# Down projection with the activations stationary, the weights moving by 512 columns, and the sample's tokens apart in plain float32

## Chip, cores and metric

The kernel runs on one core of one Trainium2 chip. The metric is device time in microseconds of that core; two runs of the kernel before gave 1352.66 and 1353.6 us, median 1353.13.

## What is computed

One layer of a streaming encoder, one step for two requests: a prompt of 256 tokens and a sample of 32 tokens, width 2048. Both go through the same weights, all float32. The mixer (gated linear attention and forgetting attention) comes first and is untouched by the change; then comes the MLP with a hidden width of 8192:

```
h = RMSNorm_pre(x);  z = h @ w_in;  ... two groups of heads ...
x = x + RMSNorm_post(concat(gla_out, fox_out) @ w_out)
x = x + RMSNorm_post2(relu(RMSNorm_pre2(x) @ w_up)^2 @ w_down)
```

`w_up` is 2048 x 8192, `w_down` 8192 x 2048. RMSNorm divides each token by the root of its mean square over the 2048 channels and multiplies by a gain per channel. The attention's keys, values, gates and states are also outputs; the change doesn't touch them.

## The kernel before

All big products have one form, `gemm` (L182). The weights come in chunks of 512 columns by 2048 rows, each in eight pieces of 256 rows (two tiles of 128 rows, `KP` = 2), through a ring of four staging tiles (`wst`, L57) that SyncE's queue fills (L141). ScalarE rounds a piece to `whi` (float32r, L160) and VectorE subtracts to get the rest, `wlo` (L161): the weights' exact value in two parts of twelve bits. The activations are split the same way. For each of four output tiles and each tile of 128 rows, TensorE runs three products out of four (L198 hi x hi, L199 hi x lo, L200 lo x hi). **The weights are the stationary operand** (128 x 128, loaded anew for every product), and the activations of all 288 tokens, prompt and sample together, are the moving one. So a chunk is 8 x 4 x 2 x 3 = 192 products of 288 columns, and the result has channels on the partitions, tokens along the row. The four accumulators are four PSUM banks (`acc`); four more banks (`aux`) serve everything else.

The MLP (L923 on) goes through the hidden width in four blocks `b`: four chunks of `w_up` (L927), whose results are squared and split to `u_hi`, `u_lo` (L940 to L943), then four chunks of `w_down` (L953), whose results VectorE adds to `dT` (L960), sixteen tiles [128 channels, 288 tokens]. With the last block, each chunk's `dT` tiles are squared and summed for the norm (L786, L791, L970, `token_sums` L230), multiplied by the gain (L981) and turned to tokens on the partitions: TensorE transposes the prompt's two tiles (L985) and multiplies the sample's 32 columns by the identity into a quarter of the partitions of `psm` (L986, one of the four column groups of the array per chunk). `finish` (L992) scales by the token's factor `rt3` and adds the residual `yN`; `store` sends the rows out.

A tile scheduler sets the order of instructions on each engine from the program text, priorities (`soon`) and its own timing; staging and splitting run two to three pieces ahead of their use.

Of the kernel before, what the change touches and what calls it, by code (L numbers as in the profile page):

```python
# [15 lines left out]
P = 128  # L16
# [26 lines left out]
def hymba_step(  # L43
# [31 lines left out]
    # ------------------------------------------------------------- constants  # L75
# [29 lines left out]
    # ---------------------------------------------------- the weights' stream  # L105
    # chunks of CW columns, in pieces of KP rows of tiles; each piece is split exactly
    # into two parts of twelve bits, and three of the four products are taken
# [21 lines left out]
    staged, sent, ready, held = {}, {}, {}, {}  # held: what a piece's split stays behind  # L129

    def stage(i):
        """The weights' piece number i on its way from DRAM."""
        if i >= NP * len(chunks) or i in staged:
            return
        src, order = chunks[i // NP]
        k0 = order[i % NP] * KP
        st = wst.tile([P, KP, CW], F32, name="wstage", tag="wstage")
        n = 1 if i == 0 else KP
        with soon() if i >= NP else nullcontext():
            for a in range(0, KP, n):  # L140
                sent[i] = nc.sync.dma_start(out=st[:, a:a + n, :], in_=src[(k0 + a) * P:(k0 + a + n) * P, :]  # L141
                                            .rearrange("(k p) c -> p k c", p=P))
        staged[i] = st
# [38 lines left out]
    def gemm(ci, a_hi, a_lo, steps=1, ahead=2):  # L182
        """NO tiles of [128 columns of the weights, T]."""
# [20 lines left out]

    def act_tiles():
        hi = [actp.tile([P, T], F32R, name=f"ah{k}", tag=f"ah{k}") for k in range(KT)]
        lo = [actp.tile([P, T], F32R, name=f"al{k}", tag=f"al{k}") for k in range(KT)]
        return hi, lo

    def rstd(tile_, ms, n, out):  # L210
        """1/sqrt(ms/n + eps) from a sum of squares: exp(-ln/2) and a Newton step."""
        v, r, t = tile_(), tile_(), tile_()
        S.activation(out=r, in_=ms, func=AF.Ln, scale=1.0 / n, bias=eps_t)
        V.tensor_scalar(out=v, in0=ms, scalar1=1.0 / n, scalar2=EPS, op0=ALU.mult, op1=ALU.add)
        S.activation(out=r, in_=r, func=AF.Exp, scale=-0.5)
        V.scalar_tensor_tensor(out=t, in0=r, scalar=-0.5, in1=v, op0=ALU.mult, op1=ALU.mult)
        V.tensor_tensor(out=t, in0=t, in1=r, op=ALU.mult)
        V.scalar_tensor_tensor(out=out, in0=t, scalar=1.5, in1=r, op0=ALU.add, op1=ALU.mult)
# [4 lines left out]
    def broadcast_tokens(r, out):  # L223
        """A number per token, [128, 3] with tokens on the partitions, to every row of a [128, T] tile."""
# [5 lines left out]
    def token_sums(pn, parts):  # L230
        """Sums over the channels of [128, T] tiles, tokens on the partitions; the sample's tokens four times."""
# [16 lines left out]
    # ------------------------------------------------------------ token mixing  # L248
    with ExitStack() as zc:
# [8 lines left out]
        # ---- the input: transposed, times its gain  # L258
# [26 lines left out]
        def add_input(q):  # L285
            """Sums of squares of 512 of the input's channels."""
# [7 lines left out]
        def warm_up(n):  # L294
            """Keeps the tensor engine's clock up while the first loads are on their way."""
# [63 lines left out]
        # the narrow columns of w_in: gate rank and forget logits  # L359
# [9 lines left out]
        # sums the four groups of partitions that the narrow columns' products go to, and puts  # L369
        # the gate's rows in three places  # L370
# [6 lines left out]
        # the gate's second factor, split like the rest, its three products in one pass over the rows  # L377
# [9 lines left out]
        # masks  # L387
# [15 lines left out]
        # gate rank, forget gates and their running sums  # L403
# [3 lines left out]
        def log_sigmoid(out, in_, bias, n0, n1, w, pool_t):  # L407
            """min(x, 0) - log1p(exp(-|x|)) of x = in_ + bias, log1p with its rounding put right."""
# [18 lines left out]
        def small_tile():  # L427
# [18 lines left out]
            # logf of the new rows, tokens on the partitions  # L446
# [11 lines left out]
            # running sums: the prompt's, and the cache's with the new rows behind  # L458
# [30 lines left out]
        def to_tokens(src, dst):  # L489
            """A [128, T] tile's transpose to a [128, 3, 128] slice, tokens on the partitions."""  # L490
# [7 lines left out]
        # ---- gated linear attention, one head  # L498
        def gla_head(h):
# [23 lines left out]
            # the first chunk's keys decayed past the second, the last chunk's queries past the  # L523
            # third, and all keys decayed to the prompt's end
# [11 lines left out]
            # att^T: keys on the partitions  # L536
# [9 lines left out]
            # queries and the keys of earlier chunks  # L546
# [21 lines left out]
            # the final states  # L568
# [10 lines left out]
            # outputs, value channels on the partitions  # L579
# [87 lines left out]
        def fox_sample(g):  # L667
            """The new rows of four heads, one head to a quadrant of partitions."""
# [56 lines left out]
        def out_gate(k, acc):  # L725
            """The normed heads times silu(r)."""
# [47 lines left out]
    # ------------------------------------------------- output projection and MLP  # L774
# [5 lines left out]
    def add_square(total, src, first):  # L780
        """total += src^2, or total = src^2."""
# [12 lines left out]
    # x and y with tokens on the partitions: two tiles of the prompt, and the sample's  # L794
    # channels in four groups
# [7 lines left out]
    yT = [mp.tile([P, T], F32, name=f"yT{k}", tag=f"y{k}") for k in range(KT)]  # L803
# [95 lines left out]
    def residual():  # L899
        """The mixer's output, brought to tokens on the partitions, plus x."""  # L900
# [21 lines left out]
    dN = None  # L922
    for b in range(NB):  # L923
        u_hi = [mp.tile([P, T], F32R, name=f"uh{k}", tag=f"uh{k}") for k in range(KT)]
        u_lo = [resp.tile([P, T], F32R, name=f"ul{k}", tag=f"r{k}") for k in range(KT)]
        for j in range(NC):
# [5 lines left out]
            for o in range(NO):  # L932
# [9 lines left out]
                S.copy(out=u_hi[k], in_=u)  # L942
                V.tensor_tensor(out=u_lo[k], in0=u, in1=u_hi[k].bitcast(F32), op=ALU.subtract)  # L943
        drain()
        if b == 0:
            dT = [mp.tile([P, T], F32, name=f"dT{k}", tag=f"y{k}") for k in range(KT)]
        if b == NB - 1:
            sac3 = mp.tile([P, T], F32, name="sac3", tag="sac", bufs=2)
            dN = [mp.tile([P, D], F32, name=f"dN{t}", tag=f"n{t}") for t in range(2)]
            psm = aux()  # L950
            last = []
        for j in range(NC):
            accs = gemm(ci, u_hi, u_lo)  # L953
            ci += 1
            for o in range(NO):
                k = NO * j + o
                if b == 0:
                    V.tensor_copy(out=dT[k], in_=accs[o][:, 0:T])
                else:
                    V.tensor_tensor(out=dT[k], in0=accs[o][:, 0:T], in1=dT[k], op=ALU.add)  # L960
            if b < NB - 1:
                continue
            for o in range(NO):
                k = NO * j + o
                if j < NC - 1:
                    add_square(sac3, dT[k], k == 0)
                else:
                    q = square(dT[k])
                    if o < NO - 2:
                        V.tensor_tensor(out=sac3, in0=sac3, in1=q, op=ALU.add)  # L970
                    else:
                        last.append(q)
            if j == NC - 1:
                pn = aux()
                token_sums(pn, [sac3] + last)
                rt3 = tok_tile()
                rstd(tok_tile, pn[:, 0:3], D, rt3)
            for o in range(NO):
                k = NO * j + o
                dg = tmp()  # L980
                V.tensor_scalar_mul(out=dg, in0=dT[k], scalar1=vcol("mpost", k))  # L981
                if o == 0:
                    pd = [aux(), aux()]
                for t in range(2):
                    PE.transpose(out=pd[t][:, o * P:(o + 1) * P], in_=dg[:, t * P:(t + 1) * P], identity=ident)  # L985
                PE.matmul(out=psm[32 * j:32 * j + DEC, o * P:(o + 1) * P], lhsT=dg[:, SEQ:T], rhs=ident,  # L986
                          start=True, stop=True)
            if j < NC - 1:
                for t in range(2):
                    S.copy(out=dN[t][:, j * CW:(j + 1) * CW], in_=pd[t])  # L990
# [26 lines left out]
    finish(V, 0, pd[0], 3)  # L1017
    store(0, 2, 2)
    finish(V, 2, psm, 0)
    for c in range(4):  # L1020
        S.dma_start(out=y_sample[0, :, c * CW:(c + 1) * CW], in_=yN[2][32 * c:32 * c + DEC, :])
    finish(V, 1, pd[1], 3)
# [28 lines left out]
```

## Time and profile before

| | |
|---|---|
| runs, median (lowest to highest) | 1353.13 us (1352.66 to 1353.6) |
| profiled execution, first to last instruction | 1353.2 us |
| TensorE busy | 1332.8 us, 98% |
| weight loads busy | 1305.4 us, 96% |
| VectorE, ScalarE, GpSimd busy | 713.0, 565.3, 151.4 us |
| moved by DMA | 217.69 MB, 161 GB/s |
| products of 288 columns, all of `gemm` | 3 x 3072 |
| of them in the down projection | 3 x 1024 |

The profiled execution's own time is its span, 1353.2 us; no other time is shown for it. TensorE's matmuls overlap in the records (each record is longer than the distance to the next), so the time of a series is read from the starts: the distance from one start to the next is what a product costs in a stream. Weight loads are records of their own that overlap the matmuls. A plain float32 product is two records, a float32r product one.

### The profile page before, as it was taken

To read this page: it belongs to the slowest core of one execution; us is meant where nothing else is said; L and a number is where in the kernel's file an instruction comes from. 1 tells how busy PE (TensorE), PEld (TensorE's weight loads), DVE (VectorE), ACT (ScalarE), POOL (GpSimd) and SP (SyncE) were. 2 spreads that over 40 slices of the span, in tenths; PEclk is the share of its full clock that TensorE was granted. 3 is DMA by queue.
4 is the path that set the end of the run, shared out by engine and by line. 5 is a ranking of instruction groups with operands and counts; after the bars stand their busy time and mean duration, and the time that the engine had idled before them with its cause. 6 is when DMAs were issued, how large, how long until landed. Compare 5 with 4: busy or idle time off the path is not lost.

```text
span 1353.2 us, 23973 instructions
## 1 busy us (share of the span) xinstructions
PE 1332.8 (98%) x9971; PEld 1305.4 (96%) x9971; DVE 713.0 (53%) x964; ACT 565.3 (42%) x872; POOL 151.4 (11%) x225
## 2 busy tenths in 40 slices
PE   9999999999999998999999999999999999999997
PEld 8999999999999987999999999999999999999996
DVE  6568565445694369544445445444444444544543
ACT  7335434334454454543333444333444333444332
POOL 2128122002113126000000000000000000000211
PEclk9999999999999999999999999999999999999998
DMA  8654355555457434555555555555555555555442
GB/s 239 182 149 133 121 178 178 173 161 159 137 164 255 156 107 120 164 170 160 168 168 161 161 168 170 158 170 166 162 172 158 160 175 162 158 171 171 140 140 70
DMA packets 115915, 217.69 MB, mean 161 GB/s; under 512 B 12044, under 2 KB 13160, under 8 KB 115552
## 3 DMA queue, kind: packets, MB, share of 16 engines
q1 hardware_dynamic: 111104, 205.75, 50.5%
q0 software_dynamic: 2624, 7.17, 1.5%
q10 hardware_dynamic: 2080, 3.25, 0.8%
q8 instruction: 78, 1.28, 0.4%
q14 instruction: 29, 0.24, 0.1%
HBM read 210.35 MB, written 5.79 MB: 160 GB/s over the span
## 4 chain that ended last, share of the span: by engine, by line
PE 95%; POOL 1%; issue 1%; DMA 1%; DVE 1%; ACT 0%; POOLq 0%; SPq 0%; DVEq 0%
PE acc L198 30%; PE acc L199 29%; PE acc L200 29%; POOL sac L787 1%; PE aux L494 1%; DMA xn<-in_x_prompt_dram 0%; POOL y L860 0%; DMA wgu<-in_w_gla_gate_up_dram 0%; PE aux L986 0%; PE aux L985 0%; PE aux L308 0%; DVE yN L909 0%; PE aux L584 0%; PE aux L634 0%; PE aux L662 0%
## 5 line engine op out<-in xcount | busy, mean ns | idle before, releaser
L161 DVE TENSOR_TENSOR wlo<-wstage,whi 128x1024 fp32r<-128x1024 f32 (+1 forms) x385 | 473.1, 1229 | 494.2 <-ACT whi L160 493.7
L160 ACT CAST whi<-wstage 128x1024 fp32r<-128x1024 f32 (+1 forms) x385 | 402.3, 1045 | 648.7 <-PE acc L199 621.6
L199 PE MATMUL acc<-al,whi 128*128 128x288 f32 x2048 | 604.3, 296 | 4.9 <-DVE al L863 4.8
L198 PE MATMUL acc<-ah,whi 128*128 128x288 f32 x2048 | 601.8, 298 | 3.7 <-ACT ah L862 1.8
L200 PE MATMUL acc<-ah,wlo 128*128 128x288 f32 x2048 | 598.9, 295 | 0.0
L199 PEld LDWEIGHTS acc<-al,whi 128*128 128x128 f32 x2048 | 385.2, 188 | 8.2 <-DVE al L863 7.2
L198 PEld LDWEIGHTS acc<-ah,whi 128*128 128x128 f32 x2048 | 381.9, 188 | 7.4 <-ACT ah L862 2.5
L200 PEld LDWEIGHTS acc<-ah,wlo 128*128 128x128 f32 x2048 | 384.7, 188 | 0.4 <-issue 0.2
L199 PE MATMUL acc<-ul,whi 128*128 128x288 f32 x1024 | 302.9, 296 | 0.0
L198 PE MATMUL acc<-uh,whi 128*128 128x288 f32 x1024 | 302.6, 296 | 0.0
L200 PE MATMUL acc<-uh,wlo 128*128 128x288 f32 x1024 | 302.3, 295 | 0.0
L199 PEld LDWEIGHTS acc<-ul,whi 128*128 128x128 f32 x1024 | 192.9, 188 | 0.6 <-issue 0.6
L200 PEld LDWEIGHTS acc<-uh,wlo 128*128 128x128 f32 x1024 | 193.1, 189 | 0.0
L198 PEld LDWEIGHTS acc<-uh,whi 128*128 128x128 f32 x1024 | 192.8, 188 | 0.0
L787 POOL TENSOR_TENSOR sac<-sac,tmp 128x288 f32<-128x288 f32 x37 | 41.8, 1129 | 814.2 <-ACT tmp L786 813.1
L940 DVE SCALAR_TENSOR_TENSOR ev<-acc,r 128x288 f32<-128x288 f32 x60 | 25.9, 452 | 27.4 <-PE acc L200 27.4
L960 DVE TENSOR_TENSOR dT<-acc,dT 128x288 f32<-128x288 f32 x48 | 20.9, 454 | 29.5 <-PE acc L200 28.6
L791 ACT ACTIVATE tmp<-ev 128x288 f32<-128x288 f32 x64 | 28.1, 442 | 14.5 <-DVE ev L940 14.5
L943 DVE TENSOR_TENSOR ul<-tmp,uh 128x288 fp32r<-128x288 f32 x64 | 26.3, 452 | 0.2 <-ACT uh L942 0.2
L942 ACT CAST uh<-tmp 128x288 fp32r<-128x288 f32 x64 | 25.7, 425 | 0.5
L341 DVE SCALAR_TENSOR_TENSOR zt<-acc,rstd 128x288 f32<-128x288 f32 x48 | 20.3, 451 | 7.6 <-PE acc L200 7.4
L860 POOL TENSOR_TENSOR y<-y,xT 128x288 f32<-128x288 f32 x13 | 17.6, 1359 | 31.9 <-DVE y L856 31.9
(296 smaller groups left out, 620.5 us busy)
## 6 DMA issues: line engine op xcount, KB each, us to landing
wstage<-in_w_mlp_up_dram SPq DMA_DIRECT2D x128, 512.0 KB, 3.8
wstage<-in_w_mlp_down_dram SPq DMA_DIRECT2D x128, 512.0 KB, 3.7
wstage<-in_w_in_dram SPq DMA_DIRECT2D x95, 512.0 KB, 3.8
wstage<-in_w_out_dram SPq DMA_DIRECT2D x32, 512.0 KB, 4.4
xN<-in_x_prompt_dram POOLq DMA_DIRECT2D x2, 1024.0 KB, 10.2
xn<-in_x_prompt_dram SPq DMA_DIRECT2D x3, 512.0 KB, 8.0
out_dram<-gst POOLq DMA_DIRECT2D x8, 128.0 KB, 2.4
kc<-in_cache_fox_k_dram ACTq DMA_DIRECT2D x2, 512.0 KB, 4.5
```

The costliest lines, as they stand in the source:

```text
L160: S.copy(out=hi[:, a:a + n, :], in_=st[:, a:a + n, :])
L161: V.tensor_tensor(out=lo[:, a:a + n, :], in0=st[:, a:a + n, :], in1=hi[:, a:a + n, :].bitcast(F32), op=ALU.subtract)
L198: PE.matmul(out=out, lhsT=hi[:, kk, sl], rhs=a_hi[k], start=(p == 0 and kk == 0), stop=False)
L199: PE.matmul(out=out, lhsT=hi[:, kk, sl], rhs=a_lo[k], start=False, stop=False)
L200: PE.matmul(out=out, lhsT=lo[:, kk, sl], rhs=a_hi[k], start=False, stop=(p == NP - 1 and kk == KP - 1))
L341: V.scalar_tensor_tensor(out=z, in0=acc[:, 0:T], scalar=scale, in1=rstd0, op0=ALU.mult, op1=ALU.mult)
L787: G.tensor_tensor(out=total, in0=total, in1=q, op=ALU.add)
L791: S.activation(out=q, in_=src, func=AF.Square)
L940: V.scalar_tensor_tensor(out=t, in0=accs[o][:, 0:T], scalar=0.0, in1=r2, op0=ALU.max, op1=ALU.mult)
L942: S.copy(out=u_hi[k], in_=u)
L943: V.tensor_tensor(out=u_lo[k], in0=u, in1=u_hi[k].bitcast(F32), op=ALU.subtract)
L960: V.tensor_tensor(out=dT[k], in0=accs[o][:, 0:T], in1=dT[k], op=ALU.add)
```

## The change

The four down chunks of each block go through a new function, `gemm_tokens`. The **activations are stationary** (`u_hi`, `u_lo` by 128 of the prompt's tokens) and the weights' split piece moves, 512 columns at a time; a chunk is 8 x 2 x 2 x 3 = 96 products of 512 columns, and the result has tokens on the partitions. The sample's 32 tokens are left out of these; they are multiplied in plain float32, without a split, straight from the staging tiles, in blocks of four products after every second piece, each of the four in its own group of 32 array columns and 32 partitions of one PSUM bank. The four partial sums are added at the end by a product with `same`, a matrix of stacked identities that GpSimd builds. The staging ring gets two more tiles (every fifth and sixth piece), since the raw piece is now read until its block. The transposes, the gain product with channels on the partitions and `token_sums` of the last norm are gone; the gain comes as a row repeated over the partitions (`gB`, `gS`), and the norm's sums come from ScalarE's squares with `accum_out`.

```diff
     def stage(i):
...
-        st = wst.tile([P, KP, CW], F32, name="wstage", tag="wstage")
+        if "pool" in raw and i % 6 >= 4:
+            st = raw["pool"].tile([P, KP, CW], F32, name="wstage2", tag="wstage2", bufs=2)
+        else:
+            st = wst.tile([P, KP, CW], F32, name="wstage", tag="wstage")
...
+    def gemm_tokens(ci, a_hi, a_lo, a_new):
+        acc, acs = [accum() for _ in range(2)], aux()
+        for p in range(NP):
...
+            for kk in range(KP):
+                k = chunks[ci][1][p] * KP + kk
+                first, final = p == 0 and kk == 0, p == NP - 1 and kk == KP - 1
+                for t in range(2):
+                    ts = slice(t * P, (t + 1) * P)
+                    PE.matmul(out=acc[t], lhsT=a_hi[k][:, ts], rhs=hi[:, kk, :], start=first, stop=False)
+                    PE.matmul(out=acc[t], lhsT=a_lo[k][:, ts], rhs=hi[:, kk, :], start=False, stop=False)
+                    PE.matmul(out=acc[t], lhsT=a_hi[k][:, ts], rhs=lo[:, kk, :], start=False, stop=final)
+            if p % 2:
+                for kk in range(2 * KP):
+                    k = chunks[ci][1][p - 1 + kk // KP] * KP + kk % KP
+                    q = 32 * kk
+                    PE.matmul(out=acs[q:q + DEC, :], lhsT=a_new[:, k, :], rhs=staged[i - 1 + kk // KP][:, kk % KP, :],
+                              start=(p == 1), stop=(p == NP - 1))
+            tick(1)
+        return acc, acs
...
                 u = square(t)
                 S.copy(out=u_hi[k], in_=u)
+                G.tensor_copy(out=u_new[:, k, :], in_=u[:, SEQ:T])
...
         for j in range(NC):
-            accs = gemm(ci, u_hi, u_lo)
+            acc, acs = gemm_tokens(ci, u_hi, u_lo, u_new)
             ci += 1
-            for o in range(NO):
-                k = NO * j + o
+            cs = slice(j * CW, (j + 1) * CW)
+            for t in range(2):
+                d = dN[t][:, cs]
                 if b == 0:
-                    V.tensor_copy(out=dT[k], in_=accs[o][:, 0:T])
+                    V.tensor_copy(out=d, in_=acc[t])
                 else:
-                    V.tensor_tensor(out=dT[k], in0=accs[o][:, 0:T], in1=dT[k], op=ALU.add)
...
-                    PE.transpose(out=pd[t][:, o * P:(o + 1) * P], in_=dg[:, t * P:(t + 1) * P], identity=ident)
-                PE.matmul(out=psm[32 * j:32 * j + DEC, o * P:(o + 1) * P], lhsT=dg[:, SEQ:T], rhs=ident,
-                          start=True, stop=True)
...
+                    V.tensor_tensor(out=d, in0=acc[t], in1=d, op=ALU.add)
+                if final:
+                    S.activation(out=junk, in_=d, func=AF.Square, accum_out=ssq[:, t, j:j + 1])
+                    (G if j < NC - 1 else V).tensor_tensor(out=d, in0=d, in1=gB[:, cs], op=ALU.mult)
+            d = dS[:, cs]
+            if b == 0:
+                S.copy(out=d, in_=acs)
+            else:
+                V.tensor_tensor(out=d, in0=acs, in1=d, op=ALU.add)
+            if final:
+                PE.matmul(out=psm[32 * j:32 * j + DEC, :], lhsT=same[:, 0:DEC], rhs=d, start=True, stop=True)
+    S.activation(out=junk, in_=psm, func=AF.Square, accum_out=ssq[:, 2, 0:1])
+    pq = aux()
+    PE.matmul(out=pq[:, 0:1], lhsT=same, rhs=ssq[:, 2, 0:1], start=True, stop=True)
...
```

Up to the first down chunk TensorE's order is the same in both kernels. There, TensorE before (L198 to L200 are `gemm`'s three products; `ah` the MLP's input, `uh` and `ul` the hidden activations):

```order
L200 MATMUL acc<-ah_5773,wlo 128x288
L198 MATMUL acc<-uh_5814,whi 128x288
L199 MATMUL acc<-ul_5830,whi 128x288
L200 MATMUL acc<-uh_5814,wlo 128x288
L198 MATMUL acc<-uh_5815,whi 128x288
```

and TensorE now (L225 to L227 are `gemm_tokens`' three products, L232 the sample's):

```order
L204 MATMUL acc<-ah_5776,wlo 128x288
L232 MATMUL aux<-wstage,u_new 32x512 x5
L225 MATMUL acc<-whi,uh_5827 128x512
L226 MATMUL acc<-whi,ul_5843 128x512
L227 MATMUL acc<-wlo,uh_5827 128x512
L225 MATMUL acc<-whi,uh_5828 128x512
...
L227 MATMUL acc<-wlo,uh_5834 128x512
L232 MATMUL aux<-wstage,u_new 32x512 x3
L225 MATMUL acc<-whi,uh_5835 128x512
```

The first two of the sample's blocks stand here as five and three products, with 48 big ones between; in the rest of the chunks a block of four stands behind every 24.

The end of VectorE's work, before (L960 adds a chunk to `dT`, L981 is the gain, L996 `finish`):

```order
L960 TENSOR_TENSOR dT_7088<-acc,dT_7088 128x288
L981 TENSOR_SCALAR tmp<-dT_7085,vec 128x288
L981 TENSOR_SCALAR tmp<-dT_7086,vec 128x288
L981 TENSOR_SCALAR tmp<-dT_7087,vec 128x288
L981 TENSOR_SCALAR tmp<-dT_7088,vec 128x288
L214 TENSOR_SCALAR tok<-aux 128x3
...
L996 SCALAR_TENSOR_TENSOR yN_4627<-dN_13378,tok,yN_4627 128x512 x3
L996 SCALAR_TENSOR_TENSOR yN_4627<-aux,tok,yN_4627 128x512
```

and now (L1013 adds to `dN`, L1021 to the sample's `dS`, L1016 and L1035 are the gain, L1031 fetches the sample's sum from TensorE, L1041 `finish`):

```order
L1013 TENSOR_TENSOR dN_7106<-acc,dN_7106 128x512
L1013 TENSOR_TENSOR dN_7107<-acc,dN_7107 128x512
L1016 TENSOR_TENSOR dN_7106<-dN_7106,gB 128x512
L1021 TENSOR_TENSOR dS<-aux,dS 128x512
L1016 TENSOR_TENSOR dN_7107<-dN_7107,gB 128x512
L1030 TENSOR_REDUCE tok<-ssqd 128x2
L1035 TENSOR_TENSOR dS<-aux,gS 128x512
L1031 COPY tok<-aux 128x1
L246 TENSOR_SCALAR tok<-tok 128x3
...
L1041 SCALAR_TENSOR_TENSOR yN_4627<-dN_7106,tok,yN_4627 128x512 x4
```

Between the last sum of a chunk and the factor `tok` there now stand a sum over the partial sums, a square and a second product.

## Rows read from the trace of the kernel before

**Rows 1.** The page, engines: busy time, share of the span, instructions.

```profile
PE 1332.8 (98%) x9971; PEld 1305.4 (96%) x9971; DVE 713.0 (53%) x964; ACT 565.3 (42%) x872; POOL 151.4 (11%) x225
```

**Rows 2.** The page, the chain that ended last, shares by engine.

```profile
PE 95%; POOL 1%; issue 1%; DMA 1%; DVE 1%; ACT 0%; POOLq 0%; SPq 0%; DVEq 0%
```

**Rows 3.** The cores: span and mean granted TensorE clock (1 is 2.4 GHz).

```profile
core 0: 1353.2 us, clock 0.994
```

**Rows 4.** Timeline, TensorE, ends of block 1's down stage: start us, length us, instruction.

```profile
817.44 0.30 PE L198 MATMUL acc<-uh,whi 128*128 128x288 f32 x1
817.57 0.29 PE L199 MATMUL acc<-ul,whi 128*128 128x288 f32 x1
...
919.57 0.29 PE L200 MATMUL acc<-uh,wlo 128*128 128x288 f32 x1
919.70 0.29 PE L198 MATMUL acc<-ah,whi 128*128 128x288 f32 x1
```

**Rows 5.** Groups by line in that stage: count, busy us, mean ns, idle before.

```profile
L200 PE MATMUL acc<-uh,wlo 128*128 128x288 f32 x256 | 75.6, 295 | 0.0
...
L161 DVE TENSOR_TENSOR wlo<-wstage,whi 128x1024 fp32r<-128x1024 f32 x32 | 39.2, 1226 | 47.9 <-ACT whi L160 47.9
L160 ACT CAST whi<-wstage 128x1024 fp32r<-128x1024 f32 x32 | 33.5, 1047 | 64.8 <-PE acc L199 64.8
```

**Rows 6.** Chain in time, plain float32 of 256 and 128 columns: start, us, count.

```profile
139.63 0.86 PE aux L571 x4
...
162.86 0.98 PE aux L494 x9
```

**Rows 7.** Timeline, TensorE, sixteen float32 products in four column groups.

```profile
71.92 0.29 PE L200 MATMUL acc<-ah,wlo 128*128 128x288 f32 x1
72.14 2.15 PE L435 MATMUL aux<-xT,wr 128*32 128x288 f32 x32
...
74.46 0.30 PE L199 MATMUL acc<-al,whi 128*128 128x288 f32 x1
```

**Rows 8.** Timeline, TensorE, four float32 products in four column groups.

```profile
284.98 0.29 PE L200 MATMUL acc<-ah,wlo 128*128 128x288 f32 x1
285.20 0.69 PE L682 MATMUL aux<-t,zt 128*32 128x288 f32 x8
...
286.06 0.29 PE L199 MATMUL acc<-al,whi 128*128 128x288 f32 x1
```

**Rows 9.** Timeline, TensorE, a chunk's transposes in the last block.

```profile
1284.30 0.30 PE L198 MATMUL acc<-uh,whi 128*128 128x288 f32 x1
1284.43 0.38 PE L985 MATMUL aux<-ident,tmp 128*128 128x128 f32 x2
1284.74 0.41 PE L986 MATMUL aux<-ident,tmp 128*32 128x128 f32 x2
...
1287.43 0.29 PE L200 MATMUL acc<-uh,wlo 128*128 128x288 f32 x1
```

**Rows 10.** Timeline, VectorE, the program's end.

```profile
1337.75 0.46 DVE L960 TENSOR_TENSOR dT<-acc,dT 128x288 f32<-128x288 f32 x1
...
1341.87 0.16 DVE L218 SCALAR_TENSOR_TENSOR tok<-tok 128x3 f32<-128x3 f32 x1
...
1342.07 3.09 DVE L996 SCALAR_TENSOR_TENSOR yN<-dN,tok,yN 128x512 f32<-128x512 f32 x3
...
1345.08 2.05 DVE L996 SCALAR_TENSOR_TENSOR yN<-aux,tok,yN 128x512 f32<-128x512 f32 x3
```

**Rows 11.** Groups by line and shape: VectorE and ScalarE on 128x512, GpSimd on 128x32.

```profile
L996 DVE SCALAR_TENSOR_TENSOR yN<-aux,tok,yN 128x512 f32<-128x512 f32 x3 | 2.1, 736 | 0.0
...
L990 ACT COPY dN<-aux 128x512 f32<-128x512 f32 x6 | 3.2, 589 | 12.7 <-PE aux L985 12.7
...
L510 POOL TENSOR_TENSOR ke<-t 128x32 f32<-128x32 f32 x4 | 2.4, 590 | 0.0
```

**Rows 12.** The page, DMA issues: KB each, us from issue to landing.

```profile
wstage<-in_w_mlp_down_dram SPq DMA_DIRECT2D x128, 512.0 KB, 3.7
```

More of the change, by code (lines that the diff above doesn't have):

```diff
@@ L127, in hymba_step @@
             chunks.append((w_down[0][b * D:(b + 1) * D, j * CW:(j + 1) * CW], low_first))
+    raw = {}
     staged, sent, ready, held = {}, {}, {}, {}
@@ L203, in gemm @@
         return accs
+    def gemm_tokens(ci, a_hi, a_lo, a_new):
+        acc, acs = [accum() for _ in range(2)], aux()
+        for p in range(NP):
+            i = ci * NP + p
+            split(i)
+            hi, lo = ready[i]
+            for n in range(1, 3):
+                stage(i + n + 1)
+                split(i + n)
+            for kk in range(KP):
[14 more added lines that the diff above has]
+        return acc, acs
     def act_tiles():
@@ L801, in hymba_step @@
         G.dma_start(out=xN[2][32 * c:32 * c + DEC, :], in_=x_sample[0, :, c * 512:(c + 1) * 512])
-    yT = [mp.tile([P, T], F32, name=f"yT{k}", tag=f"y{k}") for k in range(KT)]
+    yc = ExitStack()
+    yp = yc.enter_context(tc.tile_pool(name="yp", bufs=1))
+    yT = [yp.tile([P, T], F32, name=f"yT{k}", tag=f"y{k}") for k in range(KT)]
     sac1 = mp.tile([P, T], F32, name="sac1", tag="sac", bufs=2)
@@ L921, in hymba_step @@
     ci = nz + NC
-    dN = None
+    same = mp.tile([P, P], F32, name="same")
+    G.memset(same, 0.0)
+    for q in range(1, 8):
+        c0, n = max(0, (q - 4) * DEC), P - abs(q - 4) * DEC
+        r0 = c0 + (4 - q) * DEC
+        G.tensor_tensor(out=same[:, c0:c0 + n], in0=same[:, c0:c0 + n], in1=ident[:, r0:r0 + n], op=ALU.add)
     for b in range(NB):
+        u_new = mp.tile([P, KT, DEC], F32, name="u_new", tag="u_new")
         u_hi = [mp.tile([P, T], F32R, name=f"uh{k}", tag=f"uh{k}") for k in range(KT)]
@@ L945, in hymba_step @@
         if b == 0:
-            dT = [mp.tile([P, T], F32, name=f"dT{k}", tag=f"y{k}") for k in range(KT)]
-        if b == NB - 1:
-            sac3 = mp.tile([P, T], F32, name="sac3", tag="sac", bufs=2)
+            yc.close()
+            dp = ctx.enter_context(tc.tile_pool(name="dp", bufs=1))
+            raw["pool"] = dp
             dN = [mp.tile([P, D], F32, name=f"dN{t}", tag=f"n{t}") for t in range(2)]
+            dS = dp.tile([P, D], F32, name="dS")
+            gB = dp.tile([P, D], F32, name="gB")
@@ L950, in hymba_step @@
+            gS = mp.tile([P, CW], F32, name="gS")
+            G.dma_start(out=gB, in_=g_mlp_post.broadcast_to([P, D]))
+            for c in range(NC):
+                G.dma_start(out=gS[32 * c:32 * c + DEC, :],
+                            in_=g_mlp_post[:, c * CW:(c + 1) * CW].broadcast_to([DEC, CW]))
+        final = b == NB - 1
+        if final:
+            ssq = mp.tile([P, 3, NC], F32, name="ssqd")
+            junk = mp.tile([P, CW], F32, name="junkd", tag="n2")
             psm = aux()
-            last = []
@@ L961, in hymba_step @@
[L961 to L984, printed above, removed]
-                    PE.transpose(out=pd[t][:, o * P:(o + 1) * P], in_=dg[:, t * P:(t + 1) * P], identity=ident)
-                PE.matmul(out=psm[32 * j:32 * j + DEC, o * P:(o + 1) * P], lhsT=dg[:, SEQ:T], rhs=ident,
-                          start=True, stop=True)
@@ L988, in hymba_step @@
-            if j < NC - 1:
-                for t in range(2):
-                    S.copy(out=dN[t][:, j * CW:(j + 1) * CW], in_=pd[t])
+                    V.tensor_tensor(out=d, in0=acc[t], in1=d, op=ALU.add)
[7 more added lines that the diff above has]
+                V.tensor_tensor(out=d, in0=acs, in1=d, op=ALU.add)
@@ new lines, in hymba_step @@
+            if final:
+                PE.matmul(out=psm[32 * j:32 * j + DEC, :], lhsT=same[:, 0:DEC], rhs=d, start=True, stop=True)
+    S.activation(out=junk, in_=psm, func=AF.Square, accum_out=ssq[:, 2, 0:1])
+    pq = aux()
+    PE.matmul(out=pq[:, 0:1], lhsT=same, rhs=ssq[:, 2, 0:1], start=True, stop=True)
+    ms3 = tok_tile()
+    V.tensor_reduce(out=ms3[:, 0:2], in_=ssq[:, 0:2, :], axis=AX.X, op=ALU.add)
+    V.tensor_copy(out=ms3[:, 2:3], in_=pq[:, 0:1])
+    rt3 = tok_tile()
+    rstd(tok_tile, ms3, D, rt3)
@@ L992, in finish @@
+    dM = dS[:, 0:CW]
+    V.tensor_tensor(out=dM, in0=psm, in1=gS, op=ALU.mult)
     def finish(eng, t, src, c):
@@ L1016, in hymba_step @@
     finish(S, 1, dcol(1, 2), 2)
-    finish(V, 0, pd[0], 3)
+    finish(V, 0, dcol(0, 3), 3)
     store(0, 2, 2)
-    finish(V, 2, psm, 0)
+    finish(V, 2, dM, 0)
     for c in range(4):
         S.dma_start(out=y_sample[0, :, c * CW:(c + 1) * CW], in_=yN[2][32 * c:32 * c + DEC, :])
-    finish(V, 1, pd[1], 3)
+    finish(V, 1, dcol(1, 3), 3)
     store(1, 1, 1)
```

## The prediction, made before the changed kernel was run

> **What bounds the kernel now.** I read the page's engine list first, then the chain that ended last, then TensorE's timeline in the stage that changes. TensorE is busy for 98% of the span [rows 1] and makes up 95% of the chain [rows 2], so what a down chunk costs is the time that its instructions take on TensorE, one behind the other. The record lengths don't give that (0.29 us each, overlapped); the starts do. Block 1's down stage runs from 817.44 to 919.70 us [rows 4], 102.26 us for 3 x 256 = 768 products [rows 5], which is 133.2 ns for a product of 288 columns, with no idle time in it. The granted clock is full, 2.4 GHz [rows 3]; at one column per cycle 288 columns are 120 ns, so each product costs 13.2 ns more than its columns. The other engines have room: per piece of 3.2 us ScalarE works 1.05 and VectorE 1.23 us on the split [rows 5].
>
> **What goes.** All four blocks' down stages: 4 x 102.3 = 409.0 us. In the last block also the turning of three chunks, which stands between the products: from 1284.30 to 1287.43 us with two products of its own [rows 9], so 3.13 - 0.27 = 2.86 us, three times 8.6 us. The fourth turning lies in the tail, below.
>
> **What comes: the big products.** 16 chunks x 96 = 1536 products of 512 columns. No row shows a float32r product of another size than 288, so the price is bounded. From below, the columns at the full clock and the smallest excess that any product here shows: plain float32 takes 0.86 / 4 = 215 ns for 256 columns and 0.98 / 9 = 109 ns for 128 (L494, transposes) [rows 6], which is two cycles per column plus about 2 ns in both; 512 cycles are 213.3 ns, so 215.8. From above, the excess grows with the columns: 133.2 x 512 / 288 = 237 ns. Between them, the excess is the same for each product: 213.3 + 13.2 = 226.5 ns. I take that, since the two sizes of rows 6 carry the same excess, so where I can see two sizes it belongs to the product and not to the column. The sum: 1536 x 0.2265 = 347.9 us (331.5 to 364.0).
>
> The Trainium skill (TensorE: Matmul & The Clock Gate, Back-to-back issue gap) gives N / 2.4 + 2.5 ns when warm, about 216 ns at N = 512. It meets rows 6 when the two cycles per column are counted, but for 288 columns it says 122.5 where rows 4 have 133.2, so I don't take it for float32r; with it the big products would be 331.5 us and the whole comes out at the low end, the second rival.
>
> **What comes: the sample's blocks.** Such blocks are in the trace already. Sixteen products in four column groups, 32 records [rows 7]: from the product ahead (71.92) to the second one behind (74.46) are 2.54 us, less two ordinary distances 2.27. Four products, 8 records [rows 8]: 1.08 - 0.27 = 0.81 us. The first has eight rounds of four records side by side, the second two, so a round is (2.27 - 0.81) / 6 = 0.243 us, two cycles for each of 288 columns, and a block has 0.81 - 0.49 = 0.33 us beside its rounds, for emptying the array and loading it anew on both sides. The four groups do run at once. With 512 columns a round is 0.43 us, a block 0.86 + 0.33 = 1.19 us; 16 chunks x 4 blocks x 1.19 = 76.0 us. At the head of each down stage the order puts five and three products in place of four and four: the fifth shares the first's column group, and two more rounds are needed, 4 x 0.86 = 3.4 us. The products with `same` after the first three chunks of the last block stand beside such blocks, two rounds each: 2.6 us.
>
> **What is hidden.** The split of the weights is the same work per piece. A piece now lasts 12 x 0.2265 + 0.60 = 3.3 us instead of 3.2, and VectorE and ScalarE stay under half of it. Emptying PSUM is three operations of 128 x 512 per chunk (0.74 us on VectorE, 0.59 on ScalarE [rows 11]) where it was four of 288; two accumulators of four are used in turn, so TensorE doesn't wait for them. GpSimd's 64 copies to `u_new` are at most 0.59 us each [rows 11] on an engine that is busy 11% [rows 1]; the first block that needs the last of them stands twenty us behind. On SyncE's queue a staging tile is now freed by the sample's block, two at a time, and its next piece is due four pieces later, 13 us; landing takes 3.7 us [rows 12], 7.4 if two follow one another, cast and subtraction 2.3 us per piece. That fits. If it didn't, TensorE would wait inside the stage, in order, with all products behind it: the fourth rival.
>
> **The tail.** Before, the last sum is taken from 1337.75 us on and the tokens' factor is ready at 1342.03, 4.3 us later; then `finish` on VectorE runs until 1347.13 [rows 10]. Now from the same point: the last block (1.2 us), its sum on VectorE behind two sums and a gain product (to 2.2), the product with `same` (two rounds in turn and a load, to 3.3), the square (0.6, to 3.9), the second product and its fetch (to 4.6), the same chain for the factor (1.1, to 5.7): 1.4 us more. `finish` has six operations of SBUF operands at 1.03 us (3.09 / 3) where three read PSUM at 0.68 (2.05 / 3): 1.1 us more. Together 2.5 us, of which the last block's 1.2 us is in the 76.0 already: 1.3 us.
>
> **The sum.** 347.9 + 76.0 + 3.4 + 2.6 + 1.3 - 409.0 - 8.6 = +13.6 us. The profiled execution's time is its span, 1353.2 us, which is the runs' median (1353.1) to 0.1 us: **1367 us**, 1.0% slower, no difference that can be told: a measurement of this kernel tells about 2%, which is 27 us, 1326 to 1380.
>
> **The rivals.**
>
> *The excess goes by columns.* If float32r columns enter slower than one per cycle, 512 take 237 ns, 16.1 us more than I take: 364.0, in all +29.7, **1383 us**, slower by 2.2%. It decides from about 235 ns on. For it speaks that only float32r shows the large excess, and that float32r alone moves four bytes per cycle; against it that rows 6 show no such growth in plain float32.
>
> *The excess vanishes.* If 13.2 ns come from something that a longer product hides, 512 columns take 215.8 ns: 331.5, in all -2.8, **1350 us**, the same. For it speak rows 6, where products with the same loads carry 2 ns; against it that a transpose's neighbour follows at the same 0.13 us [rows 9], whatever is loaded next.
>
> *The load sets the distance.* If the 133.2 ns were the load of the stationary operand and the columns were free, the products would be half as many at the same price: 1536 x 0.1332 = 204.6, in all -129.7, **1223 us**. Against it, plain float32 products with a load each follow at 109 ns, and those with twice the columns at 215 [rows 6]. The Trainium skill (the same page and section) has about 131 ns at N = 512 for a stream of loads and products; rows 3 and 4 speak against it, as 288 columns alone already take as long.
>
> *A new wait.* A block that finds its raw piece not landed stops TensorE. One us in each of 64 blocks gives 1367 + 64 = **1431 us**. Nothing in rows 5 and 12 asks for it.
>
> *The groups take turns* with four different moving operands of 512 columns: 8 x 0.43 + 0.33 = 3.77 us a block, 165 us more, **1532 us**. Rows 7 have four different moving operands side by side, which speaks against it.
>
> **Chances and range.** The forecast 0.48; by columns 0.20; excess gone 0.24; load 0.01; new wait 0.05; turns 0.02. The range takes in the first three with a few us for the tail and the stages' ends: 1347 to 1385 us, which leaves out less than 0.1 by the cases and somewhat more by errors of my terms; the forecast's own range is 1360 to 1374. Faster by over 2%: 0.02, the load's case and some luck. Slower by over 2%: three quarters of the case by columns (0.15), the wait and the turns (0.07), 0.22. Within 2%: 0.76.
>
> **What would show it.** In the profile after, the distance between starts of L225 to L227 is the number that decides: 0.216, 0.227 or 0.237 us. A block of L232 should take 1.19 us from the product ahead to the one behind, by the count above, with its records in rounds of four. TensorE should have no idle time before L232 put down to DMA or to GpSimd's `u_new`. The factor `tok` should be ready 5.7 us after the last big product. I am wrong if big products and blocks both have their prices and the time is elsewhere, or if the mixer and the up projection, the same instructions in the same order, take another time.

## The result, and the profile after

The changed kernel takes 1374.88 us (median of two runs, 1374.65 and 1375.11) against 1353.13: the ratio is 1.016, 95% interval 1.013 to 1.0189. That is slower, by less than the 2% that counts as a difference here. I had forecast 1367, the right side and too little.

The page of the changed kernel: engines, then the chain's shares, then the cores.

```profile
PE 1347.1 (98%) x8857; PEld 1183.8 (86%) x8857; DVE 710.9 (52%) x931; ACT 564.4 (41%) x872; POOL 189.8 (14%) x297
...
PE 95%; DVE 1%; POOL 1%; issue 1%; DMA 0%; ACT 0%; SPq 0%; DVEq 0%; ACTq 0%; POOLq 0%
```

```profile
core 0: 1372.9 us, clock 0.995
```

TensorE has 1114 instructions fewer and is still the bound: 98% of the span, 95% of the chain, the same clock [rows 1 to 3]. Weight loads fell from 96% to 86% of the span, and that bought nothing. So the question is again what the instructions cost on TensorE, one behind the other.

Block 1's down stage of the changed kernel, by stretch (time, then each engine's busy time and count, the granted clock, DMA); the second row is block 0's, from its first big product to its last:

```profile
821.97:930.65 108.68, 108.68 (x513) 73.84 (x513) 45.59 (x47) 35.59 (x39) 1.51 (x3) 1.00 0.49 155
...
612.57:718.10 105.53, 105.53 (x494) 73.31 (x494) 42.40 (x41) 35.24 (x37) 1.02 (x2) 1.00 0.50 155
```

The stage took 102.26 us [rows 4] and takes 108.68, with TensorE busy all the time. Its two parts, from TensorE's timeline (start us, length us): a stretch of big products, and a block of the sample with its neighbours.

```profile
824.14 0.40 PE L226 MATMUL acc<-whi,ul 128*128 128x512 f32 x1
...
829.48 0.40 PE L225 MATMUL acc<-whi,uh 128*128 128x512 f32 x1
...
929.34 0.39 PE L227 MATMUL acc<-wlo,uh 128*128 128x512 f32 x1
929.65 1.07 PE L232 MATMUL aux<-wstage,u_new 128*32 128x512 f32 x8
930.65 0.40 PE L202 MATMUL acc<-ah,whi 128*128 128x288 f32 x1
930.88 0.30 PE L203 MATMUL acc<-al,whi 128*128 128x288 f32 x1
```

From 824.14 to 829.48 us lie 23 distances, 5.34 / 23 = 0.232 us for a big product. Over all 1416 such distances of the trace the mean is 231.7 ns; the 60 from the first product behind a block to the second (0.33 to 0.34 us) are left out of it, since they belong to the block. I had predicted 226.5, between 215.8 and 237. The block takes 930.88 - 929.34 = 1.54 us, less one distance of 0.232 and one of 0.133: 1.18 us, where I had 1.19.

Where TensorE waits from the first down stage to the end (engine, line, what for: us in total, times, longest):

```profile
PE aux L1023 <- DVE dS L1021: 1.2, 1, 1.2
PE aux L1028 <- ACT junkd L1026: 0.8, 1, 0.8
```

Both are in the tail. Nothing waits for a piece of weights or for `u_new`.

The tail on VectorE, to set beside [rows 10] (L1021 adds the sample's last sum, L250 makes the factor `tok`, L1041 is `finish`):

```profile
1356.37 0.68 DVE L1021 TENSOR_TENSOR dS<-aux,dS 128x512 f32<-128x512 f32 x1
...
1360.77 0.16 DVE L250 SCALAR_TENSOR_TENSOR tok<-tok 128x3 f32<-128x3 f32 x1
1361.04 4.76 DVE L1041 SCALAR_TENSOR_TENSOR yN<-dN,tok,yN 128x512 f32<-128x512 f32 x4
1365.72 1.74 DVE L1041 SCALAR_TENSOR_TENSOR yN<-dS,tok,yN 128x512 f32<-128x512 f32 x1
1367.39 0.74 DVE L1041 SCALAR_TENSOR_TENSOR yN<-dN,tok,yN 128x512 f32<-128x512 f32 x1
```

The last big product starts at 1354.48 and ends by its record at 1354.9; the factor is ready at 1360.93, 6.0 us later (predicted 5.7, before 4.3).

The sum in measured terms. Big products 1536 x 0.2317 = 355.9 us instead of 347.9, all else as predicted: 13.6 + 8.0 = +21.6 us. The runs differ by 21.75, the two profiled spans by 19.7 (1372.9 against 1353.2). The 2 us between these lie ahead of the change: the first down stage begins at 612.79 us in the trace before and at 610.74 in this one, after the same instructions. The runs of the changed kernel are about 1.7 us longer than their spans, and fifteen runs of the kernel before, taken beside the experiments below, 2.1 to 2.2 us longer than theirs. So the profiled execution of before, with a span of 1353.2, took about 1355.3 us by that difference (an estimate) and was one of the longer ones; that its time is its span, as I wrote in the forecast, was wrong. The sum doesn't hang on it, since it was added to a time that is also the runs' median.

### The profile page after: what moved, and what is told of

The parts are those of the page before. It is cut to its first block, busy times and chain, and to the rows that moved or that the text cites. A ratio compares the mean times of both kernels' runs of the same rounds, so it can differ in the third digit from the quotient of the medians.

```text
span 1372.9 us, 21851 instructions
## 1 busy us (share of the span) xinstructions
PE 1347.1 (98%) x8857; PEld 1183.8 (86%) x8857; DVE 710.9 (52%) x931; ACT 564.4 (41%) x872; POOL 189.8 (14%) x297
## 4 chain that ended last, share of the span: by engine, by line
PE 95%; DVE 1%; POOL 1%; issue 1%; DMA 0%; ACT 0%; SPq 0%; DVEq 0%; ACTq 0%; POOLq 0%
PE acc L202 20%; PE acc L204 19%; PE acc L203 19%; PE acc L225 10%; PE acc L227 9%; PE acc L226 9%; PE aux L232 5%; POOL sac L819 1%; PE aux L526 1%; DMA xn<-in_x_prompt_dram 0%; DVE yN L1041 0%; POOL y L894 0%; PE aux L340 0%; DVE yN L943 0%; PE aux L616 0%
## 5 line engine op out<-in xcount | busy, mean ns | idle before, releaser
L225 PE MATMUL acc<-whi,uh 128*128 128x512 f32 x512 | 208.3, 407 | 0.0
L226 PE MATMUL acc<-whi,ul 128*128 128x512 f32 x512 | 201.6, 394 | 0.0
L227 PE MATMUL acc<-wlo,uh 128*128 128x512 f32 x512 | 201.1, 394 | 0.0
L225 PEld LDWEIGHTS acc<-whi,uh 128*128 128x128 f32 x512 | 96.2, 188 | 69.8 <-ACT whi L164 40.2
L984 POOL COPY u_new<-tmp 128x32 f32<-128x32 f32 x64 | 33.4, 538 | 679.9 <-ACT tmp L823 679.9
L227 PEld LDWEIGHTS acc<-wlo,uh 128*128 128x128 f32 x512 | 96.5, 188 | 22.4
L226 PEld LDWEIGHTS acc<-whi,ul 128*128 128x128 f32 x512 | 96.4, 188 | 19.7
L232 PE MATMUL aux<-wstage,u_new 128*32 128x512 f32 x512 | 73.2, 604 | 0.0
L981 DVE SCALAR_TENSOR_TENSOR ev<-acc,r 128x288 f32<-128x288 f32 x60 | 25.9, 452 | 27.4 <-PE acc L204 27.4
L823 ACT ACTIVATE tmp<-ev 128x288 f32<-128x288 f32 x64 | 28.1, 442 | 15.3 <-DVE ev L981 15.3
L232 PEld LDWEIGHTS aux<-wstage,u_new 128*32 128x32 f32 x512 | 11.4, 108 | 25.7 <-issue 22.8
L819 POOL TENSOR_TENSOR sac<-sac,tmp 128x288 f32<-128x288 f32 x26 | 28.1, 1081 | 29.5 <-ACT tmp L818 28.7
```

Of the source, the lines that this page charges most:

```text
L225: PE.matmul(out=acc[t], lhsT=a_hi[k][:, ts], rhs=hi[:, kk, :], start=first, stop=False)
L226: PE.matmul(out=acc[t], lhsT=a_lo[k][:, ts], rhs=hi[:, kk, :], start=False, stop=False)
L227: PE.matmul(out=acc[t], lhsT=a_hi[k][:, ts], rhs=lo[:, kk, :], start=False, stop=final)
L232: PE.matmul(out=acs[q:q + DEC, :], lhsT=a_new[:, k, :], rhs=staged[i - 1 + kk // KP][:, kk % KP, :], start=(p == 1), stop=(p == NP - 1))
L819: G.tensor_tensor(out=total, in0=total, in1=q, op=ALU.add)
L823: S.activation(out=q, in_=src, func=AF.Square)
```

## Experiments

### What sets 231.7 ns

One kernel with several forms in its down chunks, so that the same stream is seen at seven more widths and in a second type (`widths` are the columns moved by one product, the second entry of a form is the number of tokens loaded, `halves` are the chunks of block 2's down stage):

```diff
-            acc, acs = gemm_tokens(ci, u_hi, u_lo, u_new)
+            form = {(0, 1): ((256, 256), P), (0, 2): ((384, 128), P), (0, 3): ((448, 64), P), (1, 1): ((CW,), 96),
+                    (1, 2): ((320, 192), P)}.get((b, j), ((CW,), P))
+            acc, acs = gemm_tokens(ci, u_hi, u_lo, u_new, *form)
...
+                if i // NP in halves:
+                    hi, lo = (x.bitcast(BF16)[:, :, 0:CW] for x in (hi, lo))
```

> A measuring run; the changed kernel with other shapes of the big products in some down chunks. Block 0: chunk 1 moves 2 x 256 columns in place of 512, chunk 2 384 + 128, chunk 3 448 + 64. Block 1: chunk 1 keeps 512 columns but loads 96 of each 128 tokens (the other 32 tokens of each half are left out there), chunk 2 moves 320 + 192. Block 2's down stage is in bfloat16, both parts, in place of float32r. Theory A (every float32r column takes 0.439 ns, and a product 6.7 ns beside; the line through 133.2 ns at 288 and 231.6 ns at 512): 119 ns at 256, 147 at 320, 175 at 384, 203 at 448; at 192, 128 and 64 the load shows, about 107 to 110 ns; 96 tokens change nothing, 232; bfloat16 at 512, half the bytes per column, comes down to 216. Theory B (the load of the next stationary operand takes reads from the moving one): the excess over 0.4167 ns per column is the same at all widths over 256, 13 to 18 ns, and falls by a quarter with 96 tokens, to 227 ns at 512. Theory C (the excess is on the accumulators' side): bfloat16 stays at 232.

Timeline of that kernel, TensorE (L235, L236 and L238 are the three products): stretches of 512, of 256 and of 384 and 128 columns in float32r, of 512 with 96 tokens loaded (128*96), and of 512 in bfloat16. The granted clock is 1.00 in all of them.

```profile
613.05 0.40 PE L236 MATMUL acc<-whi,ul 128*128 128x512 f32 x1
...
616.99 0.39 PE L236 MATMUL acc<-whi,ul 128*128 128x512 f32 x1
...
639.72 0.28 PE L235 MATMUL acc<-whi,uh 128*128 128x256 f32 x1
...
643.52 0.28 PE L238 MATMUL acc<-wlo,uh 128*128 128x256 f32 x1
...
668.13 0.34 PE L236 MATMUL acc<-whi,ul 128*128 128x384 f32 x1
668.31 0.34 PE L238 MATMUL acc<-wlo,uh 128*128 128x384 f32 x1
668.48 0.22 PE L235 MATMUL acc<-whi,uh 128*128 128x128 f32 x1
668.54 0.27 PE L236 MATMUL acc<-whi,ul 128*128 128x128 f32 x1
668.65 0.27 PE L238 MATMUL acc<-wlo,uh 128*128 128x128 f32 x1
668.76 0.39 PE L235 MATMUL acc<-whi,uh 128*128 128x384 f32 x1
668.99 0.34 PE L236 MATMUL acc<-whi,ul 128*128 128x384 f32 x1
...
876.53 0.47 PE L235 MATMUL acc<-whi,uh 128*96 128x512 f32 x1
876.84 0.39 PE L236 MATMUL acc<-whi,ul 128*96 128x512 f32 x1
...
881.94 0.40 PE L238 MATMUL acc<-wlo,uh 128*96 128x512 f32 x1
...
1051.05 0.38 PE L236 MATMUL acc<-whi,ul 128*128 128x512 bf16 x1
...
1056.01 0.38 PE L235 MATMUL acc<-whi,uh 128*128 128x512 bf16 x1
```

At 512 columns 17 distances make 3.94 us, 231.8 ns; at 256, 32 distances make 3.80 us, 118.8 ns. The straight line through these two is 5.8 ns + 0.441 ns per column. It gives 175.1 ns at 384, where the rows have (668.48 - 668.13) / 2 = 175; 146.9 and 203.4 at 320 and 448, where the medians of the trace are 147 and 203; and 132.9 at 288, where the kernel before has 133.2 with the roles of the operands swapped [rows 4, 5]. So a float32r product costs a little over a column's cycle for every column (0.441 ns against 0.417) and a small fixed part. Why a column costs more than its cycle, no run tells. Loading 96 tokens instead of 128 left the distance as it was: from 876.84 to 881.94 us 22 distances make 5.10 us, 231.8 ns. In bfloat16, with loads of as many columns and the same output, 23 distances make 4.96 us: 215.7 ns, that is 213.3 for the columns and 2.4.

Theory A holds. B falls with the 96 tokens, whose loads are shorter (0.16 us a record against 0.19) while the distance stays, and with an excess that grows with the width (12.1 ns at 256 columns, 18.4 at 512). Bfloat16 by itself would not decide against B, as its loads are shorter too (0.10 us). C falls with bfloat16, which writes the same accumulators.

The narrow products show where the line ends: six products (three of 384 columns, three of 128) take 668.99 - 668.13 = 0.86 us, and with 3 x 175 for the wide ones the narrow ones average 112 ns where the line has 62. The same count gives 111 ns at 192 columns and 110 at 64, so here the columns don't set the time. That the load of 128 columns does is likely, but no run changed the load of a narrow product. All big products of the two kernels are above these 0.11 us.

The Trainium skill (TensorE: Matmul & The Clock Gate, Back-to-back issue gap) has N / 2.4 + 2.5 ns for the gap of a product by itself, 215.8 at 512 columns, and the bfloat16 stream of this trace agrees with its 215.7; for float32r the 231.7 ns decide against it. The same section of the Trainium skill has a lower figure for a stream of loads and products, about 131 ns at 512 columns; it appears in no run here, where such a stream takes 215.7 ns at the least.

### What the sample costs in the new form

One block per chunk instead of four, the last one:

```diff
-            if p % 2:
+            if p == NP - 1:
```

> The changed kernel with one of the sample's four blocks per chunk (after the last piece); the other three quarters of the sample's down products are left out. Theory A (a block costs 1.19 us where it stands, and nothing else): 48 blocks and the four places with two rounds more go, 57.1 + 3.4 = 60.5 us, 1314 us, and the big products keep 231.6 ns. Theory B (the blocks also slow the products around them): more than that goes, and the big products come down to 226 ns, 8 us more, 1306 us.

Measured 1319.74 us (1318.76 to 1320.72), ratio 0.975 (0.973 to 0.9769). The big products keep their 232 ns, as A had it; B had them cheaper without blocks, and a time below A's. A's own number was 5.7 us too low, and the order says why. In each stage the scheduler placed one product of the first chunk's block ahead of the other three, so there are 20 visits to the narrow form and not 16, and a visit with one product costs the same 1.18 us as one with four, its two rounds of 0.43 us and the 0.33 beside them:

```profile
811.41 0.40 PE L226 MATMUL acc<-whi,ul 128*128 128x512 f32 x1
811.73 1.05 PE L232 MATMUL aux<-wstage,u_new 128*32 128x512 f32 x2
812.71 0.50 PE L227 MATMUL acc<-wlo,uh 128*128 128x512 f32 x1
```

From 811.41 to 812.71 less one distance the visit already has 1.07 us, and the product behind it follows 0.1 late. Four visits are 4.7 us. The three products with `same` stand beside a block in the changed kernel and apart here, 3 x 0.33 = 1.0 us. Together 5.7.

### What it cost in the old form

The kernel before, with 256 columns in seven of eight products of the down stages (`width` is 256 there):

```diff
-                out = accs[o][:, 0:T]
+                w = T if p == 0 else width
+                out = accs[o][:, 0:w]
```

> The kernel before with the sample's 32 columns left out of seven eighths of the down projection's products (256 columns move in place of 288): the price of the sample in the old form. Theory A (0.439 ns per column and 6.7 ns per product): 119.2 ns a product, 16 x 168 x 14.0 ns = 37.7 us less, 1315 us. Theory B (a fixed excess of 13.2 ns): 119.9 ns, 35.8 us less, 1317 us. Theory C (the old form is bound by its loads, 133 ns whatever moves): 1353 us, as before.

```profile
849.80 0.28 PE L199 MATMUL acc<-uh,whi 128*128 128x256 f32 x1
...
851.82 0.28 PE L201 MATMUL acc<-uh,wlo 128*128 128x256 f32 x1
```

Measured 1314.13 us (1313.68 to 1315.52), ratio 0.971 (0.9695 to 0.9724), with 17 distances in 2.02 us, 118.8 ns for 256 columns in the old form too; A and B are 1 and 3 us away, too near to each other to be told apart here, and C is out. The runs of before beside it had 1353.53, so the sample's columns cost 39.4 us in seven eighths, 45 us in all if the last eighth costs as much. The new form pays 64 x 1.18 = 75.5 us for its blocks, 3.4 for the split ones, and 2.6 for the sums with `same`.

### Fewer visits

Two blocks of eight products per chunk, with a staging ring of eight tiles:

```diff
-            if p % 2:
-                for kk in range(2 * KP):
...
-                    q = 32 * kk
+            if p % 4 == 3:
+                for kk in range(4 * KP):
...
+                    q = 32 * (kk % 4)
```

> The changed kernel with two blocks of eight sample products per chunk in place of four of four, and a staging ring of eight tiles (the gain's row is kept elsewhere for the room). Theory A (a block is 0.33 us for emptying the array and loading it anew, beside 0.43 us a round): the rounds stay, 32 times 0.33 us go, 10.6 us, 1364 us against 1375. Theory B (what a block costs is its rounds and the float32 passes alone): no change, 1375 us.

```profile
847.63 0.40 PE L227 MATMUL acc<-wlo,uh 128*128 128x512 f32 x1
847.96 1.92 PE L232 MATMUL aux<-wstage,u_new 128*32 128x512 f32 x16
849.82 0.50 PE L225 MATMUL acc<-whi,uh 128*128 128x512 f32 x1
850.15 0.39 PE L226 MATMUL acc<-whi,ul 128*128 128x512 f32 x1
```

A visit of eight products takes 850.15 - 847.63 - 2 x 0.232 = 2.06 us, 0.31 less than two of 1.18. So the price per visit is as A had it. The kernel took 1370.61 us (1370.14 to 1372.01), ratio 1.0124 (1.0107 to 1.0141): 4.3 us less than the changed kernel, not 10.6. Its trace has 39 visits where the changed kernel has 64; A had 32. 25 visits are 8.3 us; pieces of one to three products, some of them early in the up stage ahead, need six more rounds (2.6 us), and the products with `same` stand apart (1.0 us): 4.7 us by this count.

### Whether the column groups do work at once

All four products of a block in one group of 32 columns:

```diff
-                    q = 32 * kk
+                    q = 0
...
-                              start=(p == 1), stop=(p == NP - 1))
+                              start=(p == 1 and kk == 0), stop=(p == NP - 1 and kk == 2 * KP - 1))
...
```

> The changed kernel with the four products of each of the sample's blocks in the same 32 array columns and the same 32 partitions of the bank, so that they add up there; the same products, and the sum over four partial sums has one summand. Theory A (the four column groups run at once, and a block has 0.33 us beside its rounds for the change of form): a block becomes 8 rounds of 0.43 us and 0.33, 3.77 us instead of 1.20; 63 visits x 2.57 = 162 us more, 1537 us. Theory B (0.33 us is the price of switching between column groups, not of the narrow form): 3.44 us a block, 1375 + 63 x 2.24 = 1516 us. Theory C (the four operands go in one after another in both kernels, and the groups give nothing): no change, 1375 us. The big products stay at 232 ns by all three.

```profile
905.43 0.40 PE L227 MATMUL acc<-wlo,uh 128*128 128x512 f32 x1
905.76 3.62 PE L232 MATMUL aux<-wstage,u_new 128*32 128x512 f32 x8
909.31 0.50 PE L225 MATMUL acc<-whi,uh 128*128 128x512 f32 x1
909.64 0.39 PE L226 MATMUL acc<-whi,ul 128*128 128x512 f32 x1
```

1537.01 us in one run, and a block of 4.21 - 0.46 = 3.75 us: A in both. The groups save 2.57 us a block, and the 0.33 us belong to the change to the narrow form, not to having four groups.

### Type or form

The products' operands in bfloat16 parts: in block 2 of the kernel before, then in all four down stages of either kernel. The edit is the one shown first (`halves`), with `u_hi` and `u_lo` in the same type.

> The kernel before, with the operands of block 2's down stage rounded to bfloat16 parts instead of float32r parts (hi and rest, three products as ever, so less exact there); the form is the old one, 288 columns, weights stationary. Theory A (the excess of 13 ns over 288 columns belongs to float32r and goes by columns; bfloat16 pays a column per cycle and 2 to 3 ns): 122.5 ns a product, block 2's stage 768 x 0.1225 = 94.1 us instead of 102.3, 1345 us. Theory B (the excess belongs to the old form, weights loaded anew for every product, whatever the type): 133 ns, 102.3 us, 1353 us.

```profile
1059.88 0.29 PE L205 MATMUL acc<-uh,whi 128*128 128x288 bf16 x1
...
1061.96 0.29 PE L207 MATMUL acc<-uh,wlo 128*128 128x288 bf16 x1
```

17 distances in 2.08 us: 122.4 ns for 288 columns, as A had it; 1346.05 us in one run. The 13 ns that I saw in the kernel before belong to the type.

> The kernel before, with the operands of all four down stages in bfloat16 parts (hi and rest, three products as ever; two parts of eight bits where float32r's have twelve, so less exact). Theory A (a product costs what its type's columns cost, and nothing else bounds the stage): 3072 x (133.2 - 122.4) ns = 33.2 us less, 1320 us. Theory B (the pieces now come so fast, 24 x 122.4 ns = 2.94 us, that the split or the transfers bound some stages): between 1325 and 1350 us, with idle time of TensorE inside the down stages.

1321.03 us (1320.11 to 1321.49), ratio 0.9753 (0.9736 to 0.9769): A within 1 us. In the first three blocks' down stages TensorE is busy all the time (93.97 of 93.97 us in block 0), so neither the split nor the transfers bound the shorter pieces.

> The changed kernel, with the operands of the big products in all four down stages in bfloat16 parts (the sample stays plain float32; the prompt is less exact). Theory A (float32r's rate explains only the big products' 231.6 ns, and the sample's blocks are the rest): 1536 x (231.6 - 216.3) ns = 23.5 us less, 1351 us: at the kernel before, and some 31 us above the old form in the same type. Theory B (the rate is the whole reason that the change does not gain): with the same type on both sides the new form is no slower than the old one, 1320 us or less.

1345.07 us (1344.14 to 1348.84), ratio 0.9938 (0.9921 to 0.9954). B is out: at the same type the new form is 24 us slower than the old one. A had 1351; the missing 6 us are in the blocks. Block 0's stage, from its first big product to its last, as shown above for the changed kernel:

```profile
612.87:710.97 98.10, 97.39 (x484) 38.54 (x494) 41.77 (x40) 34.46 (x37) 1.01 (x2) 1.00 0.53 162
```

Between first and last lie 383 distances and 14 blocks. The changed kernel: 105.53 - 383 x 0.2317 = 16.8 us, 1.20 a block. Here: 98.10 - 383 x 0.2162 (the mean of this trace) = 15.3 us, 1.09 a block. Next to bfloat16 the change of form costs 0.1 us less, 64 visits 7 us. The traces show where it goes. Behind a block, the load and start of the first big product and the start of the second, in this kernel and then in the changed one:

```profile
840.70 0.10 PEld L235 LDWEIGHTS <-uh 128*128 128x128 bf16 x1 [0.84 <-issue]
840.70 0.39 PE L235 MATMUL acc<-whi,uh 128*128 128x512 bf16 x1
840.93 0.38 PE L236 MATMUL acc<-whi,ul 128*128 128x512 bf16 x1
```

```profile
856.37 0.19 PEld L225 LDWEIGHTS acc<-whi,uh 128*128 128x128 f32 x1 [0.84 <-issue]
856.37 0.51 PE L225 MATMUL acc<-whi,uh 128*128 128x512 f32 x1
856.71 0.40 PE L226 MATMUL acc<-whi,ul 128*128 128x512 f32 x1
```

The second product follows after 0.23 us in bfloat16, hardly more than a distance, and after 0.34 in float32r, 0.11 more than one. With 96 tokens loaded, in the kernel of the first experiment, it is 0.31 us (876.53 to 876.84), 0.08 more. The load records are 0.10, 0.19 and 0.16 us long: this part of the price follows the length of the load. Elsewhere a load runs beside the product ahead; the first behind a block starts with its own product (856.37 us both). The rest, about 0.23 us, is the same in both types.

The old form in bfloat16 parts is the version that beats both kernels, at the price of a less exact result; at float32r's precision none of these runs is faster than the kernel before.

## Why the prediction was near, and where it failed

**The bound** was read rightly: TensorE, instruction behind instruction, before and after. The measured 1374.9 us lie inside the stated range (1347 to 1385) and just above the forecast's own (1360 to 1374); it is the width of the first, drawn over three cases, that took it in, and not the reasoning on the excess.

**The big products: the step that failed.** I wrote that "the excess is the same for each product" and took 13.2 ns, because plain float32 carries the same 2 ns at two sizes [rows 6]. Plain float32 was the wrong neighbour. The excess belongs to float32r and goes mostly by columns: 13.2 ns at 288, 18.4 at 512, of which some 6 are fixed. 231.7 ns instead of 226.5 are 8.0 us, the whole miss. The rival by columns (237 ns) was off by as much the other way, since it left no fixed part.

**The blocks**, 1.19 us forecast from two blocks with 288 columns [rows 7, 8], took 1.18 to 1.20. Rounds and a fixed 0.33 us carried over to another width, to eight products in a visit and to one group; the fixed part is 0.1 us smaller next to bfloat16. That it is for emptying the array and loading it anew, as I wrote, is shown only of the load behind the block, a third of it; for the rest no run tells the reason. Turns, a load that sets the distance and a new wait were all rightly given little.

**The tail**: factor 6.0 us after the last big product (5.7), and `finish` on VectorE 7.1 us (1361.04 to 1368.13) where I had 5.1 + 1.1. From the last big product's end to the end of the span are 18.0 us; before, from the last sum on, 15.4. That is 2.6 us more against 2.5 forecast, and luck: factor and `finish` took 1.2 us more than I had, but from the end of `finish` to the end of the span are 4.8 us where before there were 6.1.

**Where the gain went.** Per chunk the prompt's 256 tokens cost (409.0 - 45) / 16 = 22.75 us with the weights stationary, the stages of before without the sample's share, and cost 96 x 231.7 ns = 22.24 us now. So to turn the product round is worth 16 x 0.51 = 8 us and 8.6 us of transposes. Against it, the sample rode along for 45 us and pays 75.5 + 3.4 + 2.6 by itself: 36.5 us more. With 1.3 us of tail the balance is +21; measured 21.75. Half as many big products in the down stages and a tenth less time of loads are worth almost nothing where columns set the price.

## What to carry to other kernels

Price a stream of products by its columns in its own type, and get the slope from two widths of that type; another type's two widths say nothing about it. Before taking a few tokens out of a wide product, ask what their columns cost there: here 32 columns more at 0.44 ns each, 14 ns in each of a chunk's 192 products, are 2.7 us a chunk, and four visits in another form 4.7. When a form has a price per visit, count the visits in the order as scheduled, not in the program's loops.

## What the runs showed of the hardware beyond this

- Float32r, at a granted clock of 1.00: 5.8 ns + 0.441 ns per column from 256 to 512 columns, at 256 and 288 in either role of the operands; bfloat16: 122.4 ns at 288 and 215.7 at 512, both the columns at 2.4 GHz and about 2.4 ns.
- A visit to the narrow form (32 columns of the array) between float32r products costs 0.33 us and its passes, whether it holds one, four or eight products and one column group or four. About 0.1 us of it lies between the first big product behind the block and the second, and that part follows the load's length: 0.11, 0.08 and 0.01 us with load records of 0.19, 0.16 and 0.10.
- Products of 64, 128 and 192 columns with a load of 128 columns each average 110 to 112 ns among wider ones, float32r.
